# Reordering one layer of a hybrid decoder: sample pooling earlier, two gates ahead of the pooling projection, spatial mixing one head at a time

## The chip, the cores and the metric

The kernel runs on all 8 cores of one Trainium2 chip. Each core takes one of eight prompts and one eighth of the sample rows; the cores don't talk to each other. The metric is device time in microseconds (us) of the slowest core. Engines are named as in the profile: PE is TensorE (matmul), DVE is VectorE, ACT is ScalarE, POOL is GpSimd.

Some executions fall in a slow state: the cores of one die, or of both, get a lower granted TensorE clock (a mean of 0.82 to 0.98 where the fast runs have 0.993 to 0.998) and the time rises by 1.5 to 19 per cent.

## The reference, cut to what matters

```python
h = rmsnorm(x, g_pre_mix)
z = h @ w_in                      # columns: a (512) | u (1024) | v (1024) | gate_a (1024) | gate_b (1024)
# branch A: trailing means over 2/4/8/16 tokens, minus the token, then a 128x128 product per group
ya = per_group_linear(trailing_mean(a) - a) * pool_scale
# branch B: chunks of 128 tokens, 8 heads of 128 channels
v  = layernorm(gelu(v))
yb = gelu(u) * (tril(W_s[h]) @ v + b_s[h])
m  = sigmoid(ga) * (ya @ w_ba) + sigmoid(gb) * (yb @ w_bb)
x  = x + rmsnorm(m @ w_out, g_post_mix)
x  = x + rmsnorm(relu(rmsnorm(x) @ w_up)**2 @ w_down, g_post_ffn)
```

There are 4 layers. A core works through three token blocks: 768 prompt tokens, 768 prompt tokens, and 512 prompt tokens with one tile of 128 sample rows (16 groups of 8 tokens, each with 15 earlier rows). So twelve block-layers run one after the other: eight of 768 tokens and four "sample layers" of 640. Each is worked in two parts, n=0 (three tiles, 384 columns) and n=1 (384 columns, or 256 in a sample layer).

## The kernel before

A Python scheduler emits instructions for the five engines and puts in the semaphore waits. What is emitted first for an engine runs first on it: in the changed kernel two sigmoids are emitted ahead of four evictions, and ScalarE starts the sigmoids at 428.63 us, the evictions at 429.39; in e6 the order is turned round, and the evictions start at 429.11, the sigmoids at 432.42. `group` emits the matmuls of one output tile into the next of eight PSUM banks, in rotation; `act_evac` has ScalarE move such a bank to SBUF through a function.

```python
# one block-layer, up to branch B (all but the first)
a_and_pooling(0)                     # a columns, then the pooling chain on DVE
u_stage(0, *subs[0])
for i in stiles[0]: v_stage(i)       # v tiles 0..2, gelu on ACT, statistics on DVE
a_and_pooling(1)                     # with the sample tile: its pooling is in here
u_stage(1, *subs[1])
pool_proj(0, *subs[0])
for i in stiles[1]: v_stage(i)
...
CH.flush(pooled[1])                  # emit what is left of the pooling chain
pool_proj(1, *subs[1])               # 4 groups of one matmul each, 4 ACT evictions (Copy, scaled)

def gate(j, n, first, step):         # 8 matmuls, then on ACT:
    ...
    act_evac(b, [("sg", q)], sgring[q][:, 0:N], ps[b][:, 0:N], AF.Sigmoid, N)

def branch_a(j, n, q):               # 4 matmuls that read all four pT(k, n)
    ...                              # then gate times product on DVE

for j in range(8):
    for n in range(2):
        q = gate(j, n, SL_GA, 1)
        branch_a(j, n, q)
    for h in ((), (0,), (1,), (2,), (3,), (4, 5), (6,), (7,))[j]:
        for n in range(2):
            spatial(h, n)            # <= 3 small matmuls, then 2 or 3 DVE passes
    ...                              # parameter loads of the next layer at j == 3
    # sample layers: one DVE pass over vsamp (128x1024) at j == 2, one at j == 4
...                                  # branch B: gates and groups over all eight heads
```

## Time and profile before

The time is 3743.42 us (median of 3 runs, 3743.28 to 3745.61).

The first part of the page: busy time and share of the span for each engine.

```profile
PE 3669.6 (98%) x22208; PEld 2101.6 (56%) x22208; DVE 1767.3 (47%) x3385; ACT 1158.8 (31%) x2528; POOL 542.1 (14%) x1220
```

TensorE is the bound. What a reordering can win is PE's 73 us of idle time, 2% of the span, and the time lost where matmuls run at half clock, which counts as busy: about 9 us here after the first 60 us, in five stretches behind gaps (read from the starts of the matmuls). The view to read first is the list of PE waits of the kernel before: who waited, on whom, total us, times, longest.

```profile
PE ps L448 <- DVE hst L440: 33.5, 6, 11.1
PE ps L391 <- DVE R L657: 12.6, 4, 3.2
PE ps L448 <- ACT R L402: 5.9, 9, 0.7
PE ps L391 <- DVE R L834: 4.9, 8, 0.9
...
PE ps L814 <- DVE R L834: 2.0, 4, 0.5
```

The first line belongs to the first 55 us, where the input is loaded. The second is the pooling projection waiting for the pooled sample block (four sample layers, 3.1 us each). The lines on R L834 are spatial mixing that has fallen behind on DVE, again in sample layers only. The third line is a transpose that finds its PSUM bank not yet evicted, 0.6 us in nine layers.

What that second line looks like in time (timeline of PE of the kernel before, second sample layer; columns: start, length, what, in brackets the idle time ahead of it and who ended it):

```profile
2950.48 0.38 PE L391 MATMUL ps<-R,wpg 128*128 128x256 bf16 x2
2954.06 0.59 PE L391 MATMUL ps<-R,wpg 128*128 128x256 bf16 x2 [3.20 <-DVE R L657]
2954.43 2.77 PE L391 MATMUL ps<-hTb,wslot 128*128 128x384 bf16 x8
2956.99 1.49 PE L391 MATMUL ps<-R,wslot 128*128 128x384 bf16 x4
```

Two projections run, two wait 3.2 us, and then the matmuls are slow: eight of 128x384 take 2.77 us, where undisturbed ones take 1.46. The windows view of the kernel before shows why. The last three columns of each line are the granted clock, the DMA share and GB/s:

```profile
2951.00:2954.00 3.00, 0.00 (x0) 0.00 (x0) 2.51 (x8) 1.06 (x3) 1.08 (x3) 0.85 0.48 76
2954.00:2957.00 3.00, 2.94 (x11) 1.47 (x12) 1.67 (x3) 0.84 (x2) 2.22 (x4) 0.50 1.06 175
...
1362.00:1365.00 3.00, 0.33 (x5) 0.14 (x3) 2.10 (x5) 0.60 (x1) 0.79 (x3) 1.00 0.49 178
1365.00:1368.00 3.00, 3.00 (x13) 1.49 (x12) 0.71 (x2) 0.49 (x1) 0.13 (x1) 0.65 0.48 190
```

After the gap the clock stands at half. The last two lines are another gap, of 2.67 us at the start of the second block.

One more line matters, from the timeline of ACT in the same layer: in every layer ScalarE has to load another function table before its first sigmoid.

```profile
2957.28 1.28 ACT L402 ACT_TABLE_LOAD   x1 [1.92 <-PE ps L391]
2958.58 0.49 ACT L402 ACTIVATE sg<-ps 128x384 bf16<-128x384 f32 x1
```

The load takes 1.28 us, and it begins only when the gate's matmuls have ended: the wait stands ahead of the load, not between the load and the sigmoid.

### The profile page before, as it was taken

To read this page: it belongs to the slowest core of one execution; us is meant where nothing else is said; L and a number is where in the kernel's file an instruction comes from. 1 tells how busy PE (TensorE), PEld (TensorE's weight loads), DVE (VectorE), ACT (ScalarE), POOL (GpSimd) and SP (SyncE) were. 2 spreads that over 40 slices of the span, in tenths; PEclk is the share of its full clock that TensorE was granted. 3 is DMA by queue.
4 is the path that set the end of the run, shared out by engine and by line. 5 is a ranking of instruction groups with operands and counts; after the bars stand their busy time and mean duration, and the time that the engine had idled before them with its cause. 6 is when DMAs were issued, how large, how long until landed. Compare 5 with 4: busy or idle time off the path is not lost.

```text
span 3742.8 us, 63960 instructions; the slowest of 8 cores (3735.5 to 3742.8 us)
## 1 busy us (share of the span) xinstructions
PE 3669.6 (98%) x22208; PEld 2101.6 (56%) x22208; DVE 1767.3 (47%) x3385; ACT 1158.8 (31%) x2528; POOL 542.1 (14%) x1220
## 2 busy tenths in 40 slices
PE   6999999999999999999999999999999999999999
PEld 3554555555455555545555554554665565665664
DVE  3642652563355256335525624642652652652652
ACT  2331332323233232323323332331332332332331
POOL 1111110211111121011101101111111111111110
PEclk9999999999999999999999999999999999999999
DMA  8684665567466566756655665685877777777773
GB/s 167 100 150 72 121 116 95 100 113 144 79 123 127 94 148 113 134 94 111 123 92 100 111 119 102 104 148 110 166 144 127 142 137 125 145 138 125 137 123 84
DMA packets 75338, 449.32 MB, mean 120 GB/s; under 512 B 9488, under 2 KB 11152, under 8 KB 29072
## 3 DMA queue, kind: packets, MB, share of 16 engines
q0 software_dynamic: 57600, 385.48, 61.0%
q1 hardware_dynamic: 17424, 59.76, 5.2%
q8 instruction: 185, 3.03, 0.3%
q14 instruction: 129, 1.06, 0.1%
HBM read 817.55 MB, written 13.10 MB: 222 GB/s over the span
## 4 chain that ended last, share of the span: by engine, by line
PE 94%; DVE 2%; issue 1%; ACT 1%; DMA 1%; POOL 1%; DVEq 0%; SPq 0%; ACTq 0%; POOLq 0%
PE ps L391 85%; PE ps L925 6%; PE ps L448 2%; PE ps L814 1%; ACT R L402 1%; DMA trilT<-c_tril 1%; DMA x<-xp 0%; DVE x L1016 0%; DVE ps L822 0%; POOL stt L418 0%; POOL stt L413 0%; ACT hst L431 0%; ACT junk L1006 0%; ACT L402 0%; DVE R L802 0%
## 5 line engine op out<-in xcount | busy, mean ns | idle before, releaser
L391 PE MATMUL ps<-hTb,wslot 128*128 128x384 bf16 (+1 forms) x11520 | 1859.1, 319 | 11.0 <-DVE hTb L454 4.2
L391 PEld LDWEIGHTS ps<-hTb,wslot 128*128 128x128 bf16 x11520 | 1122.3, 98 | 657.0 <-issue 25.4
L391 PE MATMUL ps<-wslot,R 128*128 128x512 bf16 x4352 | 947.6, 379 | 0.0
L402 ACT ACTIVATE R<-ps 128x384 bf16<-128x384 f32 (+5 forms) x1208 | 574.6, 482 | 916.6 <-PE ps L391 851.9
L391 PEld LDWEIGHTS ps<-wslot,R 128*128 128x128 bf16 x4352 | 424.1, 98 | 502.7
L943 DVE TENSOR_TENSOR R<-R 128x384 bf16<-128x384 bf16 (+1 forms) x768 | 266.3, 347 | 587.3 <-ACT R L402 585.5
L391 PE MATMUL ps<-R,wslot 128*128 128x384 bf16 (+1 forms) x2304 | 414.0, 318 | 1.3 <-DVE R L834 1.2
L312 POOL DMA_DIRECT2D wslot<-wslab x359 | 203.5, 568 | 951.9 <-PE ps L391 719.0
L402 ACT ACTIVATE sg<-ps 128x384 bf16<-128x384 f32 (+1 forms) x384 | 179.8, 471 | 491.4 <-PE ps L391 246.5
L391 PEld LDWEIGHTS ps<-R,wslot 128*128 128x128 bf16 x2304 | 225.0, 98 | 132.0 <-issue 6.7
L996 DVE TENSOR_TENSOR R<-ps,gpost 128x512 f32<-128x512 f32 x68 | 47.0, 692 | 432.2 <-ACT junk L993 432.2
L440 DVE SCALAR_TENSOR_TENSOR hst<-x,stt,gpre 128x1024 bf16<-128x1024 f32 x136 | 174.6, 1284 | 159.9 <-POOL stt L413 150.7
L925 PE MATMUL ps<-wslot,R 128*128 128x512 bf16 x1088 | 247.2, 379 | 0.0
L391 PE MATMUL ps<-wslot,hTb 128*128 128x512 bf16 x1088 | 238.6, 380 | 0.0
L431 ACT ACTIVATE hst<-x 128x1024 bf16<-128x1024 f32 x136 | 143.5, 1055 | 204.5 <-DVE x L1016 139.8
L391 PEld LDWEIGHTS ps<-wslot,hTb 128*128 128x128 bf16 x1088 | 106.4, 98 | 126.0
L993 ACT ACTIVATE junk<-ps 128x512 bf16<-128x512 f32 x68 | 40.6, 597 | 427.0 <-PE ps L391 427.0
L413 POOL TENSOR_TENSOR stt<-stt,mhalf 128x1 f32<-128x1 f32 x272 | 165.4, 608 | 40.0 <-POOL stt L435 0.5
L925 PEld LDWEIGHTS ps<-wslot,R 128*128 128x128 bf16 x1088 | 105.6, 98 | 116.4
L896 ACT ACTIVATE junk<-ps 128x512 bf16<-128x512 f32 x136 | 81.2, 597 | 270.9 <-PE ps L925 247.0
L879 DVE TENSOR_TENSOR ps<-ps,sg 128x384 f32<-128x384 f32 (+1 forms) x192 | 104.2, 542 | 126.4 <-PE ps L391 124.9
L721 DVE BATCH_NORM_STATS2 vstats<-R 128x6 f32<-128x512 bf16 x128 | 88.8, 694 | 154.0 <-ACT R L402 153.9
(75 smaller groups left out, 1824.1 us busy)
## 6 DMA issues: line engine op xcount, KB each, us to landing
wslot<-wslab POOLq DMA_DIRECT2D x359, 1024.0 KB, 15.6
x<-xp SPq DMA_DIRECT2D x16, 512.0 KB, 5.9
yp<-x SPq DMA_DIRECT2D x16, 512.0 KB, 7.2
gpre<-g_pre_m SPq DMA_DIRECT2D x12, 512.0 KB, 12.8
R<-b_sp SPq DMA_DIRECT2D x12, 512.0 KB, 13.3
gpre<-g_pre_f SPq DMA_DIRECT2D x12, 512.0 KB, 12.5
gpost<-g_pm SPq DMA_DIRECT2D x12, 512.0 KB, 15.9
gpost<-g_pf SPq DMA_DIRECT2D x12, 512.0 KB, 4.3
```

What stands on the lines that cost most here:

```text
L312: lambda e: e.dma_start(out=wslot[k][:, :], in_=wslab[l, s]), semkey=("w", k), inc=16, cost=5.7, lat=2.0)
L391: r = e.matmul(ps[b][:, 0:N], lhsT=lh, rhs=rh, start=(at + q == 0), stop=(at + q == total - 1))
L402: lambda e: e.activation(out=out, in_=in_, func=func, **kw), cost=act_us(N))
L413: lambda e: e.tensor_tensor(out=col, in0=ss, in1=mhalf[:, 0:n], op=ALU.pow))
L431: lambda e: e.activation(out=hst[q][:, :], in_=x[:, k, :], func=AF.Square, scale=1.0 / 32.0, accum_out=stt[:, i, 4:5]), cost=1.2)
L440: lambda e: e.scalar_tensor_tensor(out=hst[q][:, :], in0=x[:, k, :], scalar=stt[:, i, 5:6], in1=gpre[:, :], op0=ALU.mult, op1=ALU.mult), c ...
L448: r = e.transpose(out=pT16[:, c * 128:(c + 1) * 128], in_=hst[q][:, c * 128:(c + 1) * 128], identity=ident16[:])
L721: lambda e: e.bn_stats(out=vstats[:, i, half, :], in_=B3[:, i, cs]), cost=0.69)
L879: lambda e: e.tensor_tensor(out=ps[b][:, 0:N], in0=ps[b][:, 0:N], in1=sgring[q][:, 0:N], op=ALU.mult), cost=dve_us(N))
L896: lambda e, b=b, ci=ci: e.activation(out=junk[jq][:, 0:512], in_=ps[b][:, :], func=AF.Square, scale=1.0 / 32.0, accum_out=stt[:, i, ci:ci ...
L925: r = e.matmul(ps[b][:, :], lhsT=B2[:, k, i * 128:(i + 1) * 128], rhs=wo[:, k, :], start=(k == 0), stop=(k == 7))
L943: lambda e: e.tensor_tensor(out=fT[:, j, n0:n0 + N], in0=fT[:, j, n0:n0 + N], in1=fT[:, j, n0:n0 + N], op=ALU.mult), cost=dve_us(N, 2))
```

## The change

The intent: start the sample block's pooling so early that its projection doesn't wait; give TensorE two gates to do ahead of that projection; spread DVE's spatial-mixing work evenly; and free the parameter loads and the pooling head of waits that only the scheduler's bookkeeping asked for. No arithmetic is added or removed.

```diff
@@ parameter loads: wait for what used the space, not for each other
-            pool_dma(["raw16"] + ae, raw16, ...)
-            pool_dma(["bb16"] + ae, bb16, ...)
+            free = [(k, v) for a in ae for k, v in list(S.rd.get(a, {}).items()) + [S.lw[a]]]
+            pool_dma(["raw16"], raw16, ..., free)
+            pool_dma(["bb16"], bb16, ..., free)
...
@@ pooling head: one small DVE op for each of the 4 groups instead of one for all
-                    S.op("dve", [], head, lambda e: e.memset(aext[:, :, 0:15], 0.0), cost=0.15)
+                for g in range(4):
+                        S.op("dve", [], head, lambda e, g=g: e.memset(aext[:, g, 0:15], 0.0), cost=0.1)
...
@@ stage order
                     u_stage(0, *subs[0])
+                    if samp and l:
+                        a_and_pooling(1)
                     for i in stiles[0]:
                         v_stage(i)
-                    a_and_pooling(1)
+                    if not (samp and l):
+                        a_and_pooling(1)
                     u_stage(1, *subs[1])
+                    for q in (SL_U, SL_U + 1):
+                        release(bi, l, q)
...
-                CH.flush(pooled[1])
-                pool_proj(1, *subs[1])
...
                 for j in range(8):
+                    qs = [gate(j, n, SL_GA, 1) for n in range(2)] if j == 0 else None
+                    if j == 0:
+                        CH.flush(pooled[1])
+                        pool_proj(1, *subs[1])
                     for n in range(2):
-                        q = gate(j, n, SL_GA, 1)
-                        branch_a(j, n, q)
+                        branch_a(j, n, qs[n] if qs else gate(j, n, SL_GA, 1))
...
-                    for h in ((), (0,), (1,), (2,), (3,), (4, 5), (6,), (7,))[j]:
+                    for h in ((), (0,), (1,), (2,), (3,), (4,), (5,), (6,))[j]:
...
@@ branch B: the last head after two gates; the two vsamp passes moved here
                     if j == 0:
                         gq[0] = gate(0, n, SL_GB, 2)
+                        if n == 0:
+                            gq[1] = gate(1, n, SL_GB, 2)
+                            for nn in range(2):
+                                spatial(7, nn)
+                            gq[2] = gate(2, n, SL_GB, 2)
...
```

More of the change, by code (lines that the diff above doesn't have):

```diff
@@ L112, in ready, with dma @@
         return max(self.done.get(self.lw[k], 0.0) for k in keys) + 0.12
-    def dma(self, reads, writes, out, in_, cost=1.5, lat=2.0):
+    def dma(self, reads, writes, out, in_, cost=1.5, lat=2.0, extra=[]):
         i = self.ring
@@ L119, in dma @@
         return self.op("sp", reads, writes, lambda e: e.dma_start(out=out, in_=in_), semkey=key, inc=16,
-                       extra=(prev,) if prev[1] > 0 else (), cost=cost, lat=lat)
+                       extra=extra + ([prev] if prev[1] > 0 else []), cost=cost, lat=lat)
     def finish(self):
@@ L274, in pscol, with pool_dma @@
             return colsb[:, 32 + l * 4 + g: 32 + l * 4 + g + 1]
-        def pool_dma(writes, out, in_, cost):
+        def pool_dma(writes, out, in_, cost, extra=[]):
             key = ("g", nxt("g", 4))
             S.op("pool", [], writes, lambda e: e.dma_start(out=out, in_=in_), semkey=key, inc=16,
-                 extra=[(key, S.val[key])] if S.val[key] else (), cost=cost, lat=2.0)
+                 extra=extra + ([(key, S.val[key])] if S.val[key] else []), cost=cost, lat=2.0)
         loads = [(bi, l, s) for bi in range(len(BLOCKS)) for l in range(DEPTH) for s in range(NSLAB)]
@@ L286, in release @@
         def release(bi, l, s):
-            freed[(bi, l, s)] = S.t["pe"]
+            freed.setdefault((bi, l, s), S.t["pe"])
         def pace():
@@ L332, in stage_params @@
             raw16, bb16, bsb = par
-            pool_dma(["raw16"] + ae, raw16, w_spT[l].rearrange("p (h t) -> p h t", h=8), 1.5)
-            pool_dma(["bb16"] + ae, bb16, ln_b[l:l + 1, :].broadcast_to([128, 1024]), 1.5)
+            free = [(k, v) for a in ae for k, v in list(S.rd.get(a, {}).items()) + [S.lw[a]]]
+            pool_dma(["raw16"], raw16, w_spT[l].rearrange("p (h t) -> p h t", h=8), 1.5, free)
+            pool_dma(["bb16"], bb16, ln_b[l:l + 1, :].broadcast_to([128, 1024]), 1.5, free)
             pool_dma(["wpg"], wpg[:, :, :], w_pg[l].rearrange("p (g d) -> p g d", g=4), 0.8)
-            S.dma(after, ["bsb"] + ae, bsb.rearrange("p h t -> p (h t)"), b_sp[l:l + 1, :].broadcast_to([128, 1024]))
+            S.dma(after, ["bsb"], bsb.rearrange("p h t -> p (h t)"), b_sp[l:l + 1, :].broadcast_to([128, 1024]), extra=free)
         def load_g(key, buf, src, l):
@@ L552, in build @@
                 nsamp = has_next and BLOCKS[nbi][2]
-                head = [("aext", g) for g in range(4)] + [("og0", i) for i in range(6)]
-                if bi or l:
-                    head += ["raw16", "bb16", "bsb"]
-                if bi == 0:
-                    S.op("dve", [], head,
-                         lambda e: e.memset(aext[:, :, 0:15], 0.0), cost=0.15)
-                else:
-                    S.op("dve", [("atail", l)], head,
-                         lambda e: e.tensor_copy(out=aext[:, :, 0:15], in_=atail[:, l, :, :]), cost=0.15)
+                for g in range(4):
+                    head = [("aext", g)] + [("og0", i) for i in range(6) if 512 * i < AW * (g + 1) and AW * g < 512 * (i + 1)]
+                    if bi or l:
+                        head += ["raw16", "bb16", "bsb"]
+                    if bi == 0:
+                        S.op("dve", [], head,
+                             lambda e, g=g: e.memset(aext[:, g, 0:15], 0.0), cost=0.1)
+                    else:
+                        S.op("dve", [("atail", l)], head,
+                             lambda e, g=g: e.tensor_copy(out=aext[:, g, 0:15], in_=atail[:, l, g, :]), cost=0.1)
                 if samp:
@@ L853, in build @@
                             S.dma([], ["spst"], spst.rearrange("p g q r -> p (g q r)"), sp_in[l + 1])
-                    if samp and j == 2:
-                        S.op("dve", vk + ["gb32"], vk,
-                             lambda e: e.tensor_tensor(out=vsamp, in0=vsamp, in1=gb32, op=ALU.mult), cost=1.2)
-                    if samp and j == 4:
-                        S.op("dve", vk + ["bb32"], vk,
-                             lambda e: e.tensor_tensor(out=vsamp, in0=vsamp, in1=bb32, op=ALU.add), cost=1.2)
-                        S.dma(vk, [("svs", l)], svs[l], vsamp)
                 release(bi, l, SL_BA)
@@ L870, in branch_b @@
                         gq[0] = gate(0, n, SL_GB, 2)
-                    if j < 7:
-                        gq[j + 1] = gate(j + 1, n, SL_GB, 2)
-                    q = gq[j]
+                        if n == 0:
[3 more added lines that the diff above has]
+                            gq[2] = gate(2, n, SL_GB, 2)
+                    if j < 7 and j + 1 not in gq:
+                        gq[j + 1] = gate(j + 1, n, SL_GB, 2)
+                    if samp and n == 0 and j == 2:
+                        S.op("dve", vk + ["gb32"], vk,
+                             lambda e: e.tensor_tensor(out=vsamp, in0=vsamp, in1=gb32, op=ALU.mult), cost=1.2)
+                    if samp and n == 0 and j == 4:
+                        S.op("dve", vk + ["bb32"], vk,
+                             lambda e: e.tensor_tensor(out=vsamp, in0=vsamp, in1=bb32, op=ALU.add), cost=1.2)
+                        S.dma(vk, [("svs", l)], svs[l], vsamp)
+                    q = gq.pop(j)
                     kw, sv = slab_kn(bi, l, SL_GB + 1 + 2 * (j // 4), 8)
@@ L994, in build @@
                                                 accum_out=stt[:, i, 0:1]), cost=act_us(512) + 0.1)
-                    S.op("dve", ["gpost"], [("ps", b), ("og0", i), "raw16", "bb16", "bsb"],
+                    S.op("dve", ["gpost"], [("ps", b), ("og0", i), "raw16", "bb16", "bsb"] + [("aext", g) for g in range(4)],
                          lambda e: e.tensor_tensor(out=og0[:, i, :], in0=ps[b][:, :], in1=gpost[:, 0:512], op=ALU.mult),
@@ L1014, in ffn_chain @@
                     for co, src, key in ((0, og0[:, i, :], ("og0", i)), (512, og1[q][:, :], ("og1", q))):
-                        S.op("dve", [key, ("st", i, 3)] + [("aext", g) for g in range(4)], [("x", xk)],
+                        S.op("dve", [key, ("st", i, 3)], [("x", xk)],
                              lambda e, co=co, src=src: e.scalar_tensor_tensor(
```

## The prediction

> **What bounds the kernel.** TensorE. The page gives PE 98% busy (3669.6 of 3742.8 us); DVE has 47%, ACT 31%. Only 73 us of PE idle exist. The windows view puts 36.5 us of it in the first 55 us (input load and first norms) and about 8 at the very end; the change touches neither. The eight 768-token layers have only 0.2 to 1.2 us of PE idle each (3.5 at the second block's end). The four layers with the sample tile have 5.6 us each. So 2% (75 us) is out of reach.
>
> **What the four sample layers lose** (list of PE waits by layer):
> - 3.1 us: the last pooling projections wait for the pooled block (DVE).
> - After that gap matmuls run at half clock: windows show granted clock 0.50 to 0.64, and the first eight 128x384 matmuls take 2.65 to 2.77 us instead of 1.46. I read 1.5, 2.9, 1.7 and 1.4 us lost, mean 1.9. [...] here the clock falls 2.2 to 3.3 us into the gap, and a 2.67 us gap elsewhere cost nothing.
> - 1.7 us (0.50+0.92+0.31) behind spatial-mixing DVE work, where step 5 has two heads on top of two 1.2 us sample-v passes.
>
> Together 6.7 us, about 27 us over four layers. The remaining 0.7 us (ACT holding a PSUM bank ahead of a transpose) stays.
>
> **What the change does there.** In layers 1 to 3 of the sample block the sample pooling (about 10 us of DVE) starts some 10 us earlier and ends about 5 us before its projection: the 3.1 us and the half-clock stretch go. hT of tiles 3 and 4 is ready (2917.4) before the moved stage starts (about 2922), so nothing new waits. In layer 0 the order stays; two gates (2.2 us) cover most of the wait. One head per step leaves DVE 3.3 us of work per 3.5 us of PE: the 1.7 us should go, apart from a few tenths at the first branch-B group.
>
> **What it adds, in all twelve layers.** Order per layer becomes gate, gate, projection x4, branch-A n=0, branch-A n=1. ACT is in order: the first sigmoid needs a table load of 1.28 us that starts only after the gate's matmuls end (waits view: ACT idle 1.9 us on PE just ahead of it). Then two sigmoids (0.87 us), then four projection evictions (1.99 us at 384 columns, 1.65 at 256). From the first gate's issue end: 0.24+1.28+0.02+0.87+1.99+0.05 = 4.45 us until branch-A n=1 may start; PE arrives after 1.30+0.65+0.65 = 2.60. New PE wait: about 1.85 us in eight layers, 2.0 in three, and about 2.2 in all in sample layer 0 (part still pooling). At 1.85 us I expect no half clock.
>
> **Without effect:** removing the false order of the parameter loads, the split pooling head and the earlier slot release. No PE wait on weights appears after the start.
>
> **Sum.** 3743.4 - 27 + 8x1.85 (14.8) + 3x2.0 + 2.2 = about 3739.5 us. Range 3728 to 3753. Faster by over 2%: 0.005; within 2%: 0.985; slower: 0.01.
>
> **What shows it right or wrong.** PE waits: the pooling-projection waits gone in sample layers 1 to 3; a new wait of 1.6 to 2.1 us on an ACT eviction before the second branch-A group, once in every layer; 768-token layers longer by 1.5 to 2, sample layers shorter by about 4 to 5. Granted clock 1.0 after the first gates. The waits behind spatial mixing gone.
>
> **What would make it wrong.** If the new gap trips the clock, add 1.5 us per layer (3755). If ACT does the table load before the gate ends, about 1.3 us per layer less (3724). A DVE backlog at branch B adds a few tenths per layer.

3743.4 - 27 + 14.8 + 6.0 + 2.2 = 3739.4, "about 3739.5"; each term was read or worked out from the kernel before's trace. That no half clock follows at 1.85 us was the estimate, from the gap of 2.67 us. What is said of the clock's fall is shown: in windows of 0.2 us of the kernel before, the granted clock goes from 1.00 to 0.50 at 2.7, 2.2, 3.4 and 2.5 us after the end of the last matmul, in the four sample layers.

## The result, and the profile after

The fast runs of the changed kernel took 3736.59, 3737.55, 3737.71 and 3738.91 us. Against the fast runs of before the ratio is 0.9984, with a 95% interval of 0.9969 to 0.9998. (Ratios here are from fast runs alone; they are not quite the ratio of the medians quoted.) The forecast was 3739.5.

A change with parts in every layer moved the time by 0.16%. That isn't because nothing happened. The list of PE waits of the changed kernel:

```profile
PE ps L449 <- DVE hst L441: 36.9, 16, 10.8
PE ps L392 <- ACT R L403: 19.9, 12, 2.3
...
PE ps L392 <- DVE R L839: 0.3, 1, 0.3
```

The pooling wait (12.6 us) is gone as such, and the waits behind spatial mixing (6.9 us) have shrunk to one of 0.3. In their place stands a wait that the kernel before did not have, once in each of the twelve layers: 19.9 us on a ScalarE eviction. In the kernel before, the same place of a 768-token layer has no idle time (timeline of PE; the second branch-A group follows the next gate, at 425.66, without a gap either):

```profile
421.76 0.81 PE L391 MATMUL ps<-R,wpg 128*128 128x384 bf16 x4
422.41 1.46 PE L391 MATMUL ps<-hTb,wslot 128*128 128x384 bf16 x8
423.71 0.81 PE L391 MATMUL ps<-R,wslot 128*128 128x384 bf16 x4
```

In the changed kernel the wait looks like this (timeline of PE, then of ACT over the same stretch):

```profile
425.79 2.76 PE L392 MATMUL ps<-hTb,wslot 128*128 128x384 bf16 x16
428.39 0.81 PE L392 MATMUL ps<-R,wpg 128*128 128x384 bf16 x4
429.04 0.81 PE L392 MATMUL ps<-R,wslot 128*128 128x384 bf16 x4
431.53 0.81 PE L392 MATMUL ps<-R,wslot 128*128 128x384 bf16 x4 [1.67 <-ACT R L403]
```

```profile
426.17 0.60 ACT L403 ACTIVATE R<-ps 128x512 bf16<-128x512 f32 x1 [1.24 <-PE ps L392]
427.34 1.28 ACT L403 ACT_TABLE_LOAD   x1 [0.58 <-PE ps L392]
428.63 0.87 ACT L403 ACTIVATE sg<-ps 128x384 bf16<-128x384 f32 x2
429.39 2.00 ACT L403 ACTIVATE R<-ps,colsb 128x384 bf16<-128x384 f32 x4
```

Two gates (16 matmuls), four projections, branch A's first group, then a gap. ScalarE meanwhile loads the table, does two sigmoids and only then the four projection evictions that branch A's second group reads. A matmul of 384 columns issues every 0.1625 us here (eight in 1.30), so the first group has issued at 429.04 + 0.65 = 429.69 and the next starts at 431.53: 1.84 us lost, issue to issue. (The bracket says 1.67 because the view counts from the modelled end of the last matmul, 0.16 us after the end of issue.)

In the sample layers the same place reads:

```profile
2963.01 0.60 PE L392 MATMUL ps<-R,wpg 128*128 128x256 bf16 x4
2963.45 0.81 PE L392 MATMUL ps<-R,wslot 128*128 128x384 bf16 x4
2966.05 0.60 PE L392 MATMUL ps<-R,wslot 128*128 128x256 bf16 x4 [1.78 <-ACT R L403]
2966.48 1.47 PE L392 MATMUL ps<-hTb,wslot 128*128 128x384 bf16 x8
```

All four projections run at once, the new gap follows (2966.05 - 2964.10 = 1.95 us), and the eight matmuls after it take 1.47 us: full clock. The lengths of the layers follow, measured from the start of one stretch of up-projection to that of the next layer in the chain of waits:

| layer | before | after |
|---|---|---|
| 768 tokens | 322.4 us | 324.2 us |
| sample layer 1 to 2 | 278.75 us | 271.9 us |
| sample layer 2 to 3 | 277.4 us | 272.1 us |

Most 768-token layers pay 1.8 us each; the four sample layers gain 5 to 7. Two places differ, mainly for the clock. The first layer pays 4.1 us (336.87 instead of 332.76 from its first pooling projection to the next layer's): its new gap is 2.44 us, and the matmuls behind it ran at half clock and lost 1.7 us, on all eight cores. The step into the second block, measured the same way, pays nothing (326.64 and 326.62 us): behind the gap of 2.67 us there, six of eight cores lost 1.6 to 1.7 us to half clock in the kernel before, and none did in the changed kernel. The 96 matmuls behind that gap, before and after (timeline of PE):

```profile
1364.86 17.44 PE L391 MATMUL ps<-hTb,wslot 128*128 128x384 bf16 x96 [2.67 <-DVE hTb L454]
1374.27 15.76 PE L392 MATMUL ps<-hTb,wslot 128*128 128x384 bf16 x96 [2.67 <-DVE hTb L455]
```

### The profile page after: what moved, and what is told of

It reads as the page before. It is cut to its first block, busy times and chain, and to the rows that moved or that the text cites. A ratio compares the mean times of both kernels' runs of the same rounds, so it can differ in the third digit from the quotient of the medians.

```text
span 3736.4 us, 63847 instructions; the slowest of 8 cores (3732.5 to 3736.4 us)
## 1 busy us (share of the span) xinstructions
PE 3653.4 (98%) x22020; PEld 2096.5 (56%) x22208; DVE 1775.7 (48%) x3421; ACT 1159.8 (31%) x2528; POOL 540.8 (14%) x1220
## 4 chain that ended last, share of the span: by engine, by line
PE 93%; issue 2%; DVE 2%; ACT 1%; DMA 1%; POOL 1%; DVEq 0%; ACTq 0%; SPq 0%; POOLq 0%
PE ps L392 85%; PE ps L938 6%; PE ps L449 1%; PE ps L819 1%; ACT R L403 1%; DMA trilT<-c_tril 1%; DVE x L1029 1%; DMA x<-xp 0%; DVE hst L441 0%; ACT hst L432 0%; POOL stt L414 0%; POOL stt L419 0%; PE ps L371 0%; DVE ps L892 0%; ACT junk L1019 0%
## 5 line engine op out<-in xcount | busy, mean ns | idle before, releaser
L392 PE MATMUL ps<-wslot,R 128*128 128x512 bf16 x4252 | 939.5, 379 | 5.2
L392 PE MATMUL ps<-R,wslot 128*128 128x384 bf16 (+1 forms) x2304 | 411.4, 318 | 21.2 <-ACT R L403 19.9
L938 PE MATMUL ps<-wslot,R 128*128 128x512 bf16 x1024 | 234.8, 379 | 3.3
L424 POOL TENSOR_SCALAR stt<-stt 128x1 f32<-128x1 f32 x136 | 30.8, 226 | 879.9 <-ACT junk L909 476.9
```

Source lines behind the costliest of these rows:

```text
L392: r = e.matmul(ps[b][:, 0:N], lhsT=lh, rhs=rh, start=(at + q == 0), stop=(at + q == total - 1))
L938: r = e.matmul(ps[b][:, :], lhsT=B2[:, k, i * 128:(i + 1) * 128], rhs=wo[:, k, :], start=(k == 0), stop=(k == 7))
```

## The experiments

Ten more kernels ran. Times in the table are medians of the fast runs (a mean of two where there were two); the kernel before took between 3742.3 and 3745.6 us in the fast runs.

| run | what | fast runs, us | ratio to before |
|---|---|---|---|
| changed kernel | all parts | 3737.7 | 0.9984 |
| e1 | changed, projection ahead of the gates again | 3719.7 | 0.9936 |
| e2 | before, gates ahead of the projection alone | 3746.1 | 1.0006 |
| e3 | before, early sample pooling alone | 3727.9 | 0.9960 |
| e4 | before, spread spatial mixing alone | 3740.0 | 0.9991 |
| e5 | before, loads, head and slot release alone | 3743.2 | 0.9998 |
| e6 | changed, the gates' evictions behind the projection's | 3749.1 (one) | none |
| e7 | changed, no table load there (wrong result) | 3732.9 (two) | none |
| e8 | a version built from the readings | 3714.7 | 0.9921 |
| e9 | changed, second gate behind the projection | 3736.4 | 0.9979 |
| e10 | as e9, no table load there (wrong result) | 3720.6 | 0.9939 |

The 95% intervals of the ratios of e2 (0.9982 to 1.0030), e4 (0.9973 to 1.0008), e5 (0.9983 to 1.0012) and e9 (0.9936 to 1.0022) include 1. What is said of e2, e4 and e9 rests on their waits and on the lengths of their layers, not on the total; of e5 it can only be said that no effect on the total shows.

### e1: the projection ahead of the gates again

```diff
+                CH.flush(pooled[1])
+                pool_proj(1, *subs[1])
                 for j in range(8):
-                    qs = [gate(j, n, SL_GA, 1) for n in range(2)] if j == 0 else None
-                    if j == 0:
-                        CH.flush(pooled[1])
-                        pool_proj(1, *subs[1])
                     for n in range(2):
-                        branch_a(j, n, qs[n] if qs else gate(j, n, SL_GA, 1))
+                        branch_a(j, n, gate(j, n, SL_GA, 1))
```

> The changed kernel with one part undone: the second pooling projection stands ahead of the first two gates again, as before. Theory (the sigmoid table load, two sigmoids and four evictions queue in ScalarE ahead of branch A's second group): the wait on an ACT eviction of 1.7 to 1.8 us goes from all twelve layers, 768-token layers get about 1.8 us shorter (324.2 to 322.4), sample layers 1 to 3 about 1.9 shorter; sample layer 0 gets its pooling wait of 3.1 us and a half-clock stretch back (about 3.4 us). Sum: 3738 - 20.5 + 3.4 = about 3721 us. Rival (the wait is not the order of ScalarE but the projection's own latency, or a slot or bank shortage of the new order): a wait of about the same size stays ahead of branch A and the time stays within 3 us of 3738.

Measured: 3719.7 us. No wait on an ACT eviction is left in the list of PE waits; 768-token layers are back at 322.4 us; the one pooling wait that stays is sample layer 0's, 3.1 us. The rival falls: the wait came with the order of the two gates and the projection, the only thing undone here. This part of the change costs 18 us inside the changed kernel.

### e2: the gates ahead of the projection, alone

```diff
+                    qs = [gate(j, n, SL_GA, 1) for n in range(2)] if j == 0 else None
+                    if j == 0:
+                        CH.flush(pooled[1])
+                        pool_proj(1, *subs[1])
                     for n in range(2):
-                        q = gate(j, n, SL_GA, 1)
-                        branch_a(j, n, q)
+                        branch_a(j, n, qs[n] if qs else gate(j, n, SL_GA, 1))
```

> The kernel before with only the first two gates moved ahead of the pooling projection. Theory: every 768-token layer gets 1.8 us longer (+14.7 in all); the four sample layers lose the long gap: two short waits of about 1 us each in place of 3.1, no half clock after them, about 3 us shorter each (-12.5). Sum: about 3746 us, between 3743 and 3749. Rival (moving the gates is what makes the changed kernel faster): below 3740 us.

Measured: fast runs of 3745.7 to 3748.9 us, ratio 1.0006; 768-token layers 324.2 us. The sample layers have two waits, 1.0 us on a sigmoid and 0.5 us on an eviction, where one of 3.1 us stood, and take 274.4 us (before: 278.75 and 277.4). Alone, this part about breaks even: it hides a late pooling in four layers and adds a gap in eight. Once the pooling is early in three of the four sample layers, little is left to hide, and mostly the price remains. That is why it costs about 3 us here, which the interval does not tell from nothing, and 18 us in e1.

### e3: the early sample pooling, alone

```diff
+                    if samp and l:
+                        a_and_pooling(1)
                     for i in stiles[0]:
                         v_stage(i)
-                    a_and_pooling(1)
+                    if not (samp and l):
+                        a_and_pooling(1)
```

> The kernel before with only the sample block's second pooling stage moved ahead of its first v tiles, in layers 1 to 3. Theory: the 3.1 us wait and the half-clock stretch (1.4 to 2.9 us) go from three layers and stay in sample layer 0: 5 us each, about 3728 us; 768-token layers unchanged to 0.1 us. Rival (an earlier start does not end earlier, because VectorE works on bn statistics in between, or the stage then waits for transposes): over half of the 3.1 us stays or a new wait on hT shows; above 3736 us.

Measured: 3727.9 us, ratio 0.9960. One pooling wait of 3.1 us is left (sample layer 0), sample layers take 272.35 us, 768-token layers 322.4. This one move is worth about 15 us, more than the whole change.

### e4: spatial mixing spread, alone

```diff
-                    for h in ((), (0,), (1,), (2,), (3,), (4, 5), (6,), (7,))[j]:
+                    for h in ((), (0,), (1,), (2,), (3,), (4,), (5,), (6,))[j]:
...
+                        if n == 0:
+                            gq[1] = gate(1, n, SL_GB, 2)
+                            for nn in range(2):
+                                spatial(7, nn)
+                            gq[2] = gate(2, n, SL_GB, 2)
```

(cut: the two vsamp passes are moved into branch B, and a gate already emitted isn't emitted again, as in the change)

> The kernel before with only the spatial mixing spread (one head per step, the last in branch B) and the two sample-v passes moved to branch B. Theory: the three waits behind spatial mixing (0.50+0.92+0.31 and their latencies, about 2 us per sample layer) go, 8 us in all; the last head in branch B costs each 768-token layer about 0.2 us (+1.8). Sum: about 3737.5 us. Rival (the waits were a backlog that began with the pooling, not the doubled head): the waits stay within a third and the time is above 3741.

Measured: 3740.0 us, between the two forecasts. The waits behind spatial mixing did go (6.9 us became one of 0.4), so the rival falls, and 768-token layers grew by 0.2 us as expected. What is missing is about 2.5 us, and a loss of that size lies in the half-clock stretch, which this experiment should have left alone. The chain of waits shows the stretch from the end of each pooling gap to the next piece, the same 50 matmuls in all four sample layers, in the kernel before:

```profile
2677.01 8.36 PE ps L391 x50
...
2954.06 9.76 PE ps L391 x50
...
3232.73 8.65 PE ps L391 x50
...
3510.09 8.25 PE ps L391 x50
```

and in e4:

```profile
2678.37 8.71 PE ps L391 x50
...
2953.56 9.74 PE ps L391 x50
...
3230.02 9.75 PE ps L391 x50
...
3506.56 9.72 PE ps L391 x50
```

The same 50 matmuls take 7.04 us where the clock stays up. The sum of the four is 35.0 us in one and 37.9 in the other, so 2.9 us went into slower clocks after the same gaps. Over all cores: the sums of the kernel before lie between 33.6 and 35.2 us, those of e4 between 37.9 and 38.1 on six cores, at 33.7 on one and at 29.9 on one, and that last core also has the shortest span of the eight (3730.8 us against 3734.4 to 3738.6). After a gap of 3.1 us the clock stays at 0.50 for longer or shorter in the kernel before: for 3.4 us in 22 of the 32 stretches, for 6.8 us in eight, and in two it does not fall at all. What sets the length is not shown.

### e5: loads, head and slot release, alone

The first and second blocks of the diff of the change and the earlier `release`, on the kernel before.

> The kernel before with only the parameter loads without false order, the pooling head split by group and the earlier release of two weight slots. Theory (no wait on weights or parameters shows, so none can go; only the 0.6 us wait of a transpose on an ACT eviction, which depends on the head, shrinks to 0.3 as it did in the changed kernel): 9 x 0.25 us, about 3741.5 us, inside 3740 to 3744. Rival (the parameter loads held up VectorE or the weights): below 3738 us.

Measured: 3741.35 to 3744.45 us, ratio 0.9998 (0.9983 to 1.0012): no effect on the time shows. The 768-token layers did get 0.2 us shorter, as forecast (322.16 us from projection to projection, 322.39 in the kernel before). The transpose's wait did shrink, from 0.6 on ACT to 0.4 on DVE in a 768-token layer, and one of the spatial waits grew from 0.5 to at most 0.8. The false order of the parameter loads cost TensorE nothing that shows in its waits.

### e6: the gates' sigmoids behind the projection's evictions

```diff
-                    qs = [gate(j, n, SL_GA, 1) for n in range(2)] if j == 0 else None
+                    later = []
+                    qs = [gate(j, n, SL_GA, 1, later) for n in range(2)] if j == 0 else None
                     if j == 0:
                         CH.flush(pooled[1])
                         pool_proj(1, *subs[1])
+                        for ev in later:
+                            ev()
```

(`gate` with a list appends its eviction to it and does not emit it)

> The changed kernel with the evictions of the first two gates issued behind those of the projection; the matmul order stays. Theory (one in-order ScalarE queue and eight PSUM banks): the four projection evictions no longer queue behind the table load, so the wait at branch A's second group falls from 1.84 us (issue to issue) to about 1.1; but the sigmoids then run about 1.7 us later and the third gate finds its bank, that of the first gate, still unread: a new wait of about 1.2 us. Together about 2.3 us: 768-token layers 324.5 to 325.0 us, time about 3741 to 3743. Rival (only the eviction ahead of branch A counts): the wait falls to 1.1 or less and nothing new shows, 3728 to 3730 us.

Measured: one fast run of 3749.1 us. Both predicted waits are there (timeline of PE of e6, then of ACT):

```profile
429.34 0.81 PE L392 MATMUL ps<-R,wslot 128*128 128x384 bf16 x4
431.25 0.81 PE L392 MATMUL ps<-R,wslot 128*128 128x384 bf16 x4 [1.10 <-ACT R L403]
433.05 1.46 PE L392 MATMUL ps<-hTb,wslot 128*128 128x384 bf16 x8 [0.99 <-ACT sg L403]
```

```profile
429.11 1.99 ACT L403 ACTIVATE R<-ps,colsb 128x384 bf16<-128x384 f32 x4 [2.06 <-PE ps L392]
431.12 1.28 ACT L403 ACT_TABLE_LOAD   x1
432.42 0.87 ACT L403 ACTIVATE sg<-ps 128x384 bf16<-128x384 f32 x2
```

The first gap shrank to 431.25 - 429.99 = 1.26 us, and the third gate then waited for the first gate's sigmoid to free its PSUM bank (eight groups later, the same bank). Moving the sigmoids away from the place where they hurt made them hurt one group later. A 768-token layer takes 324.8 us, as expected. The total is 6 us over the forecast, and the trace shows most of that. On the profiled core the matmuls behind the two gaps were slow in four layers: the first, the fourth (326.5 instead of 324.8 us, eight matmuls in 2.27 us, a granted clock of 0.57 over 4 us) and two sample layers. The 24 matmuls behind the gaps took 5.74 us in the first and the fourth, against 4.06 in the other 768-token layers, and 5.10 and 5.01 us in the two sample layers, against about 3.4 (the same 24 in e9); together about 6.5 us lost, where the changed kernel has one such stretch of 1.7. There is one fast run, but the undisturbed dies of the three slow runs took about as long (3742.4 to 3747.7 us).

### e7: without the table load (wrong result)

```diff
-                    qs = [gate(j, n, SL_GA, 1) for n in range(2)] if j == 0 else None
+                    qs = [gate(j, n, SL_GA, 1, AF.Gelu_apprx_tanh) for n in range(2)] if j == 0 else None
```

(cut: `gate` takes the function of its eviction as an argument)

> The changed kernel with a wrong result on purpose: the first two gates of branch A are evicted with the gelu that ScalarE already has loaded, so the table load comes only with the third gate. Theory: the table load is 1.28 us of the 1.84: the wait falls to 0.5 to 0.6 us issue to issue, 768-token layers 322.9 to 323.0, time about 3738 - 12 x 1.28 = 3723 us. Rival (the two sigmoids and four evictions alone fill the wait, the load is hidden under the second gate): less than 0.5 us per layer, above 3732.

Measured: 3731.8 and 3733.9 us. The theory's number fell here: 3723 was expected. In a layer (timeline of PE, then of ACT, of e7):

```profile
426.65 0.81 PE L392 MATMUL ps<-R,wslot 128*128 128x384 bf16 x4
428.78 0.81 PE L392 MATMUL ps<-R,wslot 128*128 128x384 bf16 x4 [1.32 <-ACT R L403]
```

```profile
426.26 0.49 ACT L403 ACTIVATE sg<-ps 128x384 bf16<-128x384 f32 x1 [0.81 <-PE ps L392]
426.65 1.99 ACT L403 ACTIVATE R<-ps,colsb 128x384 bf16<-128x384 f32 x4
```

The load of 1.28 us is gone, the gap is still 428.78 - 427.30 = 1.48 us, and ACT was idle for 0.81 us ahead of the second sigmoid. A 768-token layer takes 323.87 us instead of 324.22: the load was worth 0.35 us, not 1.28. Without it, what holds branch A up is the way through the second gate: its matmuls, then its eviction at 426.26, then, without idle time, the four evictions of 2.0 us, against the projection and a single branch-A group of 0.65 us each. The way through the projection alone is hardly shorter: in e6, with no gate's eviction ahead, the four start 0.42 us after the projection's first matmul, here 0.65. Counted from the end of issue of the first gate, branch A's second group starts 428.78 - 424.70 = 4.08 us later here and 4.44 with the load. With that the first theory falls. The new one is that the wait is the longer of two paths (the text below has the second begin at the projection); e9 and e10 test it against the rival that the parts simply add.

### e9 and e10: the second gate behind the projection, with and without the table load

```diff
-                    qs = [gate(j, n, SL_GA, 1) for n in range(2)] if j == 0 else None
+                    qs = [gate(j, 0, SL_GA, 1)] if j == 0 else None
                     if j == 0:
                         CH.flush(pooled[1])
                         pool_proj(1, *subs[1])
+                        qs.append(gate(j, 1, SL_GA, 1))
```

> The changed kernel with the second gate behind the projection instead of ahead of it (gate, projection x4, gate, branch-A n=0, n=1). The run without the table load showed that removing 1.28 us of load saves only 0.36: there must be a second path of nearly the same length, from the projection's matmuls through their own four evictions (about 2.2 us) against one branch-A group of 0.65 us. New theory (the wait is the longer of two paths: ScalarE's queue through the load, and projection to eviction): with the gate behind, the second path gets 1.3 us more cover, so only the queue counts: 0.24+1.28+0.02+0.43+1.99+0.05 = 4.0 after the gate, TensorE arrives after 2.6: wait about 1.4 us issue to issue, 768-token layers 323.8, about 3733 us. Rival (the parts add up, and the load is worth 0.36 wherever it stands): the wait falls by the whole 1.3 us to about 0.5, 3723 us.

Measured for e9: 3733.9 to 3737.9 us. Timeline of PE of e9:

```profile
426.80 1.46 PE L392 MATMUL ps<-hTb,wslot 128*128 128x384 bf16 x8
428.10 0.81 PE L392 MATMUL ps<-R,wslot 128*128 128x384 bf16 x4
430.20 0.81 PE L392 MATMUL ps<-R,wslot 128*128 128x384 bf16 x4 [1.29 <-ACT R L403]
```

> The same order as the run before, and with a wrong result on purpose the first two gates evicted with the loaded gelu. New theory (longer of two paths): with the load gone and the gate behind, both paths are short: first eviction can start 0.67 us after the gate, four take 1.99: 2.7 against 2.6, wait 0.0 to 0.2 us at 384 columns and about 0.4 in sample layers; 768-token layers 322.5 to 322.7, about 3719 us. So the load that was worth 0.36 in the changed order is worth about 1.3 here. Rival (parts add up): the load is again worth 0.36, wait near 1.0 with the other run at 1.4.

Measured for e10 (wrong result, as e7): 3720.6 us. Timeline of PE of e10, where the two branch-A groups are one line of eight, 1.64 us long instead of 1.46:

```profile
424.74 1.46 PE L392 MATMUL ps<-hTb,wslot 128*128 128x384 bf16 x8
426.04 1.64 PE L392 MATMUL ps<-R,wslot 128*128 128x384 bf16 x8
```

Length of a 768-token layer in the four cases (from the chain of waits):

| | with the load | without |
|---|---|---|
| both gates ahead (changed kernel, e7) | 324.22 | 323.87 |
| one gate behind (e9, e10) | 323.84 | 322.57 |

Taking the load away saves 0.35 us in the first row and 1.27 in the second; moving the gate saves 0.38 in the first column and 1.30 in the second. Added up, the two would save 0.73; together they save 1.65. The parts do not add. The gap is the longer of two paths that nearly tie, and shortening either alone wins next to nothing. The rival falls. (The time of e9 came out 3 us above its forecast, while its 768-token layers were right to 0.1 us and its gap, 430.20 - 428.75 = 1.45 us, to 0.05. A part of the 3 us is shown: the 96 matmuls behind the 2.67 us gap at the start of the second block took 18.36 us in e9 and 15.60 in the changed kernel, from which the forecast was reckoned; and sample layer 0 waits 1.8 us on a sigmoid, for which the forecast had no term. The rest stays open.)

### e8: a version built from the readings

```diff
+                hold = samp and l == 0
+                if not hold:
+                    CH.flush(pooled[1])
+                    pool_proj(1, *subs[1])
                 for j in range(8):
-                    qs = [gate(j, n, SL_GA, 1) for n in range(2)] if j == 0 else None
-                    if j == 0:
+                    qs = [gate(j, n, SL_GA, 1) for n in range(2)] if j == 0 and hold else None
+                    if j == 0 and hold:
...
-                    for h in ((), (0,), (1,), (2,), (3,), (4,), (5,), (6,))[j]:
+                    for h in ((), (0,), (1,), (2,), (3,), (4,) if samp else (4, 5), (5,) if samp else (6,), (6,) if samp else (7,))[j]:
...
-                        if n == 0:
+                        if n == 0 and samp:
```

> The version built from the readings: early sample pooling, loads and head as changed; the projection ahead of the gates in all layers but sample layer 0, where the gates stay first; the spread of spatial mixing only in sample layers. Theory: as the run with the projection first (3719.5), less 8 x 0.2 us (branch B's first group waits for no spatial head in 768-token layers) and less about 3 us (sample layer 0 without the long gap): about 3715 us, 0.992 to 0.993 of before. Rival (the gates-first order in sample layer 0 costs what it saves): 3718 us.

Measured: fast runs of 3713.5, 3714.7 and 3715.1 us, ratio 0.9921 (0.9905 to 0.9938), correct. That is within 1 us of the forecast sum of the parts, 29 us under the kernel before and 23 under the changed one. The two terms beyond e1 show in the layers (first pooling projection to first pooling projection): 322.2 us for 768 tokens, 322.4 in e1, and 271.8 us from sample layer 0 to 1, 275.9 in e1. Its profiled run fell in the slow state on one die; on the other die, undisturbed, the cores took 3708.1 to 3713.0 us, and the one read there has two short waits of 0.9 and 0.6 us in sample layer 0 and none at this place in the other layers.

## Why the prediction was right

The prediction said 3739.5 us; the fast runs have a median of 3737.7. It held because it summed two large terms of opposite sign, each from durations in the trace. That it held to 2 us is in part luck: two effects of the clock that the sum does not have cancelled each other, 1.7 us lost behind the new gap of the first layer and 1.7 us no longer lost behind the gap at the second block.

- **What bounds it, and that 2% is out of reach.** Right: PE stays at 98% busy.
- **The sample layers' gain.** Right in kind: the pooling wait is gone in layers 1 to 3 (e3 shows the move does it), the spatial waits are gone (e4), the clock reads 1.00 behind the new gap. The size was a little low: "shorter by about 4 to 5" was 6.9 and 5.3. Two of the reasons are shown: the bracketed waits leave out 0.16 us each of matmul tail, and layer 1's half-clock stretch was the longest (9.76 us where 7.04 is full clock, 2.7 lost).
- **The new wait in all twelve layers.** Right, with the sum: 4.45 us from the first gate's issue end was forecast; measured 431.53 - 427.09 = 4.44, against an arrival after 2.60. The gap was 1.84 (forecast 1.85) in 768-token layers and 1.95 (forecast 2.0) in sample layers. e1 shows that the gates' place is the cause. In sample layer 0 two waits of 0.9 and 0.5 us replaced 3.1.
- **A few tenths at the first branch-B group.** Right: e4's 768-token layers are 0.2 us longer.
- **Loads, head, slot release without effect.** Right in time (e5, 0.9998). One detail was off: the prediction let the 0.7 us wait ahead of a transpose "stay", and it shrank to 0.3 or 0.4.
- **"If ACT does the table load before the gate ends, about 1.3 us per layer less (3724)".** Wrong, and not visible in the total. The forecast summed the longest path and did not work out the second one. The measurement in its place is e7: with no load at all the layer shortens by 0.35 us and the time is 3733. The step that failed is the silent one, that a path's term can be taken off the wait in full.
- **"A 2.67 us gap elsewhere cost nothing".** Wrong for the kernel before, of which it was said. The windows view shows the clock at 0.65 in the 3 us after that gap, and the 96 matmuls behind it took from 1364.86 to 1382.14, 17.28 us, where 96 x 0.1625 = 15.6: 1.7 us lost. The merged line of 96 matmuls hid it. (In the changed kernel the same gap did cost nothing, on any core.) The conclusion drawn from it, no half clock after 1.85 us, still held in the layers at hand (gap of 1.84 us, granted clock 1.00). In the very first layer the new gap was longer (2.3 us in the view, as ScalarE's four evictions took 2.60 us there instead of 2.00), and the eight matmuls after it took 2.63 us: half clock again, a loss that was not in the sum.

## What to carry to other kernels

Work put ahead of a stage to hide its wait brings its own tail on an engine that works its queue in order (here 1.28 us of table load and 0.87 us of sigmoids ahead of the four evictions on ScalarE): count what it queues in front of the very results that the next step needs, and do it for every layer that gets the new order, not only for those that had the wait. Before a term is taken off a wait, work out the second-longest path to the same instruction; where two nearly tie, shortening one wins little, and only an experiment with both shows what each is worth. A change of several parts that moves the time little should be taken apart: here one part alone won 0.4%, and another inside the same change lost 0.5%.

## What the traces of this case show of the clock, the issue of matmuls and the table load

- Half clock (a granted clock of 0.50) followed the gaps of 3.1 us in the kernel before in 30 of 32 cases (four layers, eight cores; the 50 matmuls took 8.19 to 9.79 us, where 7.04 is full clock), its gap of 2.67 us on six of eight cores (1.7 us lost in 96 matmuls), and the gap of 2.44 us in the first layer of the changed kernel on all eight (1.7 us lost). In e6, on the profiled core, a pair of gaps of 1.26 and 1.15 us was followed by slow matmuls in one of the seven later 768-token layers (a granted clock of 0.57 over 4 us, 1.7 us lost). Half clock did not follow the gap of 2.67 us in the changed kernel on any core, nor the gaps of 1.84 us in its seven later 768-token layers (eight matmuls in 1.46 or 1.47 us on all eight cores). So the length of the gap alone does not decide in these traces. The clock can also fall after the gap has ended (0.65 in the 3 us behind the one of 2.67).
- In the fast runs all eight cores had a mean granted clock of 0.993 to 0.998; in the slow runs a slowed die had between 0.82 and 0.98.
- In the stretches read here a matmul of 384 columns issues every 0.1625 us (eight in 1.30), and one of 512 columns every 0.216 (48 in 10.36).
- A table load takes 1.28 us, and no further time for the switch shows: in e6 the load starts 0.02 us after the eviction ahead of it ends, and the sigmoid 0.02 us after the load.
- The load waited for the data of the function that needed it: in the four sample layers of the kernel before ScalarE was idle for 1.80 to 1.95 us, waiting for the gate's matmuls, right ahead of the load.
